# The last down product of a decoder layer: two token parts of 280 and 240 columns, and GpSimd kept out of the second

## The chip, the core and the metric

The kernel runs on one core of one Trainium2 chip, as one launch. The metric is device time in microseconds (us) of that launch, the median of several runs; lower is better. A profiled execution also leaves a trace, whose span runs from the first to the last instruction. The engines are TensorE (PE in the profile, PEld for its weight loads), VectorE (DVE), ScalarE (ACT), GpSimd (POOL) and SyncE (SP), which issues transfers. A queue is shown with a q behind the engine's name.

## The reference, cut to what matters

One layer of a decoder trunk is computed for 512 prompt tokens and 8 sample tokens that share all weights. Its end is the gated feed-forward part and a final norm over the 1024 features:

```python
h2 = rms_norm(x, norm2_g) * (1.0 + sc2) + sh2
gu, up = jnp.split(h2 @ w_ffn_in, 2, axis=-1)
x = x + g2 * ((jax.nn.silu(gu) * up) @ w_ffn_out)
...
y = rms_norm(x, normf_g)      # x / sqrt(mean(x*x) + EPS) * g
```

The gate `g2` is one vector for the prompt and a vector of its own for each of the 8 samples. All is float32.

## The kernel before, in words

Everything is held transposed: features on the 128 partitions, the 520 tokens (512 of the prompt, then 8 samples) along the columns. `x` is eight tiles of 128 features by 520 tokens. Each matrix product is made in a split form: the weights are a high and a low part (`whi`/`wlo`, or `whs`/`wls` where they lie in the general heap), the activations too (`ach`/`acl`), both in the type float32r, and three TensorE matmuls per block of 128 inputs make the product (high by high, low by high, high by low; line 281). A product of 520 columns doesn't fit one bank of PSUM, so the columns are taken in `HALVES` of 260 and 260.

The feed-forward part is done in four sections of inner blocks (`SECT`); the last has five blocks (17 to 21). At its end stands the last down product, `by_halves("fo", ...)` at line 1640: for the half j=0 all eight output tiles i=0..7, then for j=1 all eight. One output tile of one half is 5 x 3 = 15 matmuls, so a half has 120. `begin` and `split_upto` split the weights of the eight units ahead of use, ACT making the high part (line 226) and DVE the low part (line 228).

After each product `fo_done(i, j, b)` follows:

- `residual` adds the gated product to `x`. The first half is one DVE instruction over 260 columns (line 1392). The second half is one over 252 prompt columns (line 1396) and two of 8 columns for the samples (lines 1399 and 1400).
- `sum_squares` squares the new `x` on ACT (line 372; the first tile straight into the sum, line 369) and adds the square to `ss3` on POOL for i below 5, else on DVE (line 373). In the second half the squares of tiles 6 and 7 are not added; TensorE takes them as matmul inputs of their own.
- Where POOL will make the tile's `y`, ACT first scales `x` in place with the norm's weight (line 1494): every tile of the first half, tiles 1, 3 and 5 of the second.

`fo_between(j)` makes the norm of a half. For the first half it is called after the product of tile 0 of the second half: a matmul with ones sums over the partitions (line 380), ACT takes the root (line 381), DVE the reciprocal (line 382), and POOL multiplies all eight tiles (line 1518), with three stores to `yT` (line 1522). For the second half, after the last product: matmuls at line 1509, root at 1510, reciprocal into a PSUM bank at 1512, an ACT copy of it to SBUF at 1513 (GpSimd's products read that copy), five products on DVE (line 1520), three on POOL (line 1518), and four stores. Stores go through SP's queue.

The order on each engine is set by a scheduler that goes by the order of the program text and by what it takes to be ready; each engine then runs its list in order and waits on semaphores. At the end of the kernel each engine drains and all meet at a barrier; the profile books these instructions at line 1691, where the tile context ends.

Of the kernel before, what the change touches and what calls it, by code (L numbers as in the profile page):

```python
# [8 lines left out]
F32 = mybir.dt.float32  # L9
F32R = mybir.dt.float32r  # L10
I32 = mybir.dt.int32
AF = mybir.ActivationFunctionType
ALU = mybir.AluOpType
# [4 lines left out]
D = 1024  # L18
NP = 512
NS = 8  # L20
NT = NP + NS
# [3 lines left out]
KT = 8  # L25
# [2 lines left out]
EPS = 1e-6  # L28
HALF = NT // 2
HALVES = ((0, HALF), (HALF, NT))  # L30

COL_XR, COL_GR, COL_Q, COL_K, COL_V = 0, 1024, 2048, 3072, 4096
COL_FL, COL_GA, COL_GB = 5120, 5136, 6160

P_N1, P_N2, P_NF, P_CW, P_CB, P_BR, P_BI, P_LAM = 0, 1, 2, 3, 7, 8, 9, 10
# [29 lines left out]
def kernel(ctx, tc, xT, par, gates, b_f, cst, cse, own, cache_k, cache_v, cache_lf, pt,  # L65
# [3 lines left out]
    pe, act, dve, pool, sp = nc.tensor, nc.scalar, nc.vector, nc.gpsimd, nc.sync  # L69
# [9 lines left out]
    def slot(name, cols=NT, dt=F32, parts=128):  # L79
        return heap.tile([parts, cols], dt, name=name, tag="slot")  # L80

    def bank(name, parts=128, cols=512):
        return psp.tile([parts, cols], F32, name=name, tag="bank")

    def small(name, parts, cols, bufs=4):
        return sm.tile([parts, cols], F32, name=name, tag="s_" + name, bufs=bufs)
# [6 lines left out]
    x = []  # L93
# [169 lines left out]
    def begin(last=None):  # L263
        n = state["n"]
        state["n"] += 1
        last = len(units) - 1 if last is None else last
        if n < 42:
            tick(KEYS[n], n in VALUES)
        load_chunks(units[reach(n, last, state["load"])][0])
        split_upto(reach(n, last, state["lead"]))  # L270
        flush()
        return n

    def half_product(n, j, a, out):
        hi, lo = splits[n]
        nk = units[n][2]
        t0, t1 = HALVES[j]
        for k in range(nk):
            ah, al = a(k, j) if callable(a) else (v[:, t0:t1] for v in a[k])
            for m, (wt, at) in enumerate(((hi, ah), (lo, ah), (hi, al))):  # L280
                state["mm"] = pe.matmul(out[:, :HALF], lhsT=wt[k], rhs=at, start=k == 0 and m == 0,  # L281
                                        stop=k == nk - 1 and m == 2)

    def run_later(n):
# [81 lines left out]
    def sum_squares(name, f, acc, src, j, eng=dve):  # L366
        t0, t1 = HALVES[j]
        if f == 0:
            act.activation(acc[:, t0:t1], src[:, t0:t1], AF.Square)
        else:  # L370
            q_ = heap.tile([128, HALF], F32, name=name, tag="slot")
            act.activation(q_, src[:, t0:t1], AF.Square)
            eng.tensor_tensor(acc[:, t0:t1], acc[:, t0:t1], q_, ALU.add)  # L373

    def rstd_half(name, ssum, r, j, more=()):
        t0, t1 = HALVES[j]
        ps = bank(f"{name}_{j}")
        parts = [ssum[:, t0:t1], *more]
        for n, q_ in enumerate(parts):
            pe.matmul(ps[:, :HALF], lhsT=ones, rhs=q_, start=n == 0, stop=n == len(parts) - 1)  # L380
        act.activation(r[:, t0:t1], ps[:, :HALF], AF.Sqrt, bias=eps, scale=1.0 / D)
        dve.reciprocal(r[:, t0:t1], r[:, t0:t1])
# [1007 lines left out]
    def residual(f, ps, gate, j):  # L1390
        if j == 0:
            dve.scalar_tensor_tensor(x[f][:, :HALF], ps[:, :HALF], mod[:, gate, f, 0:1], x[f][:, :HALF],
                                     ALU.mult, ALU.add)
            return
        n = NP - HALF
        dve.scalar_tensor_tensor(x[f][:, HALF:NP], ps[:, :n], mod[:, gate, f, 0:1], x[f][:, HALF:NP],  # L1396
                                 ALU.mult, ALU.add)
        t = small("rs", 128, NS)
        dve.tensor_tensor(t, ps[:, n:HALF], mod[:, gate, f, 1:9], ALU.mult)
        dve.tensor_tensor(x[f][:, NP:], x[f][:, NP:], t, ALU.add)  # L1400
# [37 lines left out]
    def by_halves(name, a, done, between):  # L1438
        u = state["n"]
        for j in range(2):  # L1440
            for i in range(KT):
                if j == 0:
                    begin(u + KT - 1)
                b = bank(f"{name}{i}_{j}")
                half_product(u + i, j, a, b)
                done(i, j, b)
                if j == 1 and i == 0:
                    between(0)
                if j == 1 and i < 4 and u + KT < len(units):
                    load_chunks(units[u + KT + i][0])  # L1450
                    split_upto(u + KT + i)
# [24 lines left out]
        t0, t1 = HALVES[j]  # L1476
        dve.tensor_tensor(t[:, t0:t1], b[:, :HALF], t[:, t0:t1], ALU.mult)  # L1477

    tail = []

    def on_pool(f, j):
        return j == 0 or f in (1, 3, 5)

    def fo_done(i, j, b):
        residual(i, b, 5, j)
        if j == 0 or i < 6:
            sum_squares("sq3", i, tail[0], x[i], j, pool if i < 5 else dve)
        else:
            q_ = heap.tile([128, HALF], F32, name="sq3", tag="slot")
            act.activation(q_, x[i][:, HALF:], AF.Square)  # L1490
            squares.append(q_)
        if on_pool(i, j):
            t0, t1 = HALVES[j]
            act.activation(x[i][:, t0:t1], x[i][:, t0:t1], AF.Copy, scale=prm[:, i, P_NF:P_NF + 1])

    squares = []

    def fo_between(j):
        r3 = tail[1]
        t0, t1 = HALVES[j]  # L1500
        r = r3[:, t0:t1]
        if j == 0:
            rstd_half("r3", tail[0], r3, j)
        else:

            ps = bank("r3_1")
            parts = [tail[0][:, t0:t1], *squares]
            for n, q_ in enumerate(parts):
                pe.matmul(ps[:, :HALF], lhsT=ones, rhs=q_, start=n == 0, stop=n == len(parts) - 1)
            act.activation(r, ps[:, :HALF], AF.Sqrt, bias=eps, scale=1.0 / D)  # L1510
            rp = bank("r3p")[:, :HALF]
            dve.reciprocal(rp, r)
            act.copy(r, rp)
        for f0, f1 in ((0, 2), (2, 5), (5, 8)) if j == 0 else ((0, 2), (2, 4), (4, 6), (6, 8)):
            y = pgp.tile([128, 3, HALF], F32, name="y", tag="pg")
            for f in range(f0, f1):
                if on_pool(f, j):
                    pool.tensor_tensor(y[:, f - f0], x[f][:, t0:t1], r, ALU.mult)
                else:
                    dve.scalar_tensor_tensor(y[:, f - f0], x[f][:, t0:t1], prm[:, f, P_NF:P_NF + 1],  # L1520
                                             rp if j else r, ALU.mult, ALU.mult)
            sp.dma_start(yT[128 * f0:128 * f1, t0:t1].rearrange("(f p) t -> p f t", p=128), y[:, :f1 - f0])

    def pair_out():
        return slot("ach", dt=F32R), slot("acl", dt=F32R)
# [75 lines left out]
    for sec, (j0, j1) in enumerate(SECT):  # L1601
        ac = []
        if j0 == 0:
            ts = [slot("sw") for _ in range(PLAIN)]
            ready = []
            u = state["n"]
            for j in range(2):
                for m in range(2 * PLAIN):
                    if j == 0:
                        begin(u + 3)  # L1610
                    b = bank(f"fi{m}_{j}")
                    half_product(u + m, j, h2, b)
                    ready.append((times_up if m % 2 else swish, b, ts[m // 2], j))
                    if j == 0 and m == 0:
                        rstd_half("r2", ss2, r2, 1)
                    if j or m:
                        for fn, *args in ready:
                            fn(*args)
                        ready.clear()
                    if j == 0 and m == 0:  # L1620
                        h2_half(1)
                    first = u + 2 * PLAIN
                    if j == 0:
                        load_chunks(units[first + m][0])
                    elif m:
                        split_upto(first + m - 1)
            for t in ts:
                out = pair_out()
                split_part(out, t)
                ac.append(out)  # L1630
        for jt in range(max(j0, PLAIN), j1):
            if jt == PLAIN:
                for k in range(4):
                    h2_blocks(k)
                defer(0, lambda: split_blocks(0))
                defer(1, lambda: split_blocks(2))
            ac.append((fast_tile if jt in FAST else ffn_tile)(jt))
        if j1 == FF // 128:
            tail += [slot("ss3"), slot("r3")]
            by_halves("fo", ac, fo_done, fo_between)  # L1640
            fo_between(1)
        else:
            for i in range(KT):
                product(f"fo{sec}_{i}", ac, lambda j, b: residual(i, b, 5, j))
# [62 lines left out]
```

## Time and profile before

| | |
|---|---|
| time, median of 3 runs | 1046.94 us (1045.0, 1046.94, 1053.59) |
| time of the profiled execution | 1044.21 us |
| its span | 1042.3 us |
| TensorE clock granted | 0.991 of full speed |
| TensorE busy | 998.9 us (96%) |
| VectorE / ScalarE / GpSimd busy | 777.5 / 533.2 / 304.0 us |

The profiled execution is 1.9 us longer than its span, which lies outside the first and last instruction. Times inside the profile are counted from the start of the span. The chain of waits follows the work that ended last backwards; the timeline lists an engine's instructions in order with start, duration and, in square brackets, the idle time before and what ended it; groups give a mean duration. The ends of matmuls are modelled, so their starts are the better measure.

### The profile page before, as it was taken

How to read it: one execution, taken by the hardware profiler on the slowest of the kernel's cores; microseconds unless marked ns; L12 is line 12 of the kernel's file. 1: busy time of each engine (PE TensorE's matmuls, PEld its weight loads, DVE VectorE, ACT ScalarE, POOL GpSimd, SP SyncE). 2: the span in 40 equal slices, each digit the busy share in tenths (PEclk: the TensorE clock that was granted, in tenths of full speed). 3: DMA queues.
4: the chain of work that ended last, by engine and by line, in shares of the span. 5: the costliest groups of instructions: out<-in, count | busy, mean ns of one | idle time of the engine just before them, and what ended most of it. 6: DMA issues, size and time to landing. Idle time of an engine off the chain costs nothing.

```text
span 1042.3 us, 21246 instructions
## 1 busy us (share of the span) xinstructions
PE 998.9 (96%) x8054; PEld 925.8 (89%) x8054; DVE 777.5 (75%) x1370; ACT 533.2 (51%) x1072; POOL 304.0 (29%) x411
## 2 busy tenths in 40 slices
PE   4999999999999999999999999899999999999993
PEld 1888899999898988878888989899999999999993
DVE  5447999988989978886665546778589558869663
ACT  4523665857671467767793234555244324524451
POOL 0224411112133235654500003472224033223113
PEclk9999999999999999999999999999999999999997
DMA  9898987787889999996766863132343234143212
GB/s 326 295 306 289 300 281 216 262 253 270 263 253 309 321 326 284 303 274 213 263 230 209 282 226 82 41 82 75 100 111 83 91 111 121 54 128 102 75 52 83
DMA packets 165353, 206.97 MB, mean 199 GB/s; under 512 B 9842, under 2 KB 126082, under 8 KB 165186
## 3 DMA queue, kind: packets, MB, share of 16 engines
q1 hardware_dynamic: 148530, 152.52, 47.2%
q0 software_dynamic: 13040, 46.67, 13.5%
q10 hardware_dynamic: 3680, 6.42, 1.7%
q8 instruction: 63, 1.03, 0.4%
q14 instruction: 40, 0.33, 0.1%
HBM read 192.49 MB, written 13.09 MB: 197 GB/s over the span
## 4 chain that ended last, share of the span: by engine, by line
PE 70%; DVE 12%; DMA 7%; ACT 5%; issue 4%; POOL 1%; SPq 0%; POOLq 0%; DVEq 0%; ACTq 0%
PE fo L281 11%; PE fi_S L1578 7%; PE fi_A L1578 5%; PE pb L281 4%; PE gb L281 4%; PE fig L281 4%; PE fiu L281 4%; PE ga L281 3%; PE k L281 3%; PE wo L281 3%; PE v L281 3%; DVE wlo L228 2%; PE gr L281 2%; PE xr L281 2%; DMA wraw<-in_w_in_dram 2%
## 5 line engine op out<-in xcount | busy, mean ns | idle before, releaser
L226 ACT CAST whi<-wraw 128x1024 fp32r<-128x1024 f32 (+2 forms) x113 | 111.4, 987 | 186.1 <-PE fo L281 45.0
L228 DVE TENSOR_TENSOR wlo<-wraw,whi 128x1024 fp32r<-128x1024 f32 (+2 forms) x113 | 137.3, 1216 | 48.6 <-ACT whi L226 40.9
L281 PE MATMUL fo<-ach,whi 128*128 128x260 f32 x302 | 85.6, 283 | 0.0
L281 PE MATMUL fo<-ach,wlo 128*128 128x260 f32 x302 | 85.2, 282 | 0.0
L281 PE MATMUL fo<-acl,whi 128*128 128x260 f32 x302 | 85.0, 282 | 0.0
L658 POOL DMA_DIRECT2D pg<-in_cache_k_dram x74 | 39.4, 533 | 142.4 <-DVE S L707 70.5
L241 POOL TENSOR_TENSOR ws<-wraw 128x512 f32<-128x512 f32 x13 | 20.0, 1538 | 193.5 <-DMA wraw<-in_w_fi_dram 188.7
L706 DVE TENSOR_TENSOR pg<-pg,qb 128x1024 f32<-128x1024 f32 x48 | 58.0, 1227 | 2.4 <-DMA pg<-in_cache_k_dram 2.4
L707 DVE TENSOR_REDUCE S<-pg 128x16 f32<-128x1024 f32 x48 | 57.0, 1207 | 0.1
L281 PEld LDWEIGHTS fo<-ach,whi 128*128 128x128 f32 x302 | 56.8, 188 | 0.2
L281 PEld LDWEIGHTS fo<-ach,wlo 128*128 128x128 f32 x302 | 56.8, 188 | 0.0
L281 PEld LDWEIGHTS fo<-acl,whi 128*128 128x128 f32 x302 | 56.8, 188 | 0.0
L1191 POOL TENSOR_SCALAR p<-p,mu 128x128 f32<-128x128 f32 (+3 forms) x28 | 35.9, 1293 | 48.2 <-DVE mu L1187 31.6
L249 DVE TENSOR_TENSOR wb<-ws,wb 128x512 fp32r<-128x512 f32 x52 | 45.8, 891 | 4.2 <-ACT wb L248 4.1
L373 POOL TENSOR_TENSOR ss<-ss,sq 128x260 f32<-128x260 f32 x18 | 13.7, 761 | 111.3 <-PE ada L344 58.9
L248 ACT CAST wb<-ws 128x512 fp32r<-128x512 f32 x52 | 31.5, 619 | 26.2 <-PE fi_S L1578 8.6
L1185 ACT ACTIVATE p<-p,mu 128x128 f32<-128x128 f32 (+3 forms) x64 | 35.3, 552 | 15.8 <-DVE mu L1184 15.5
L248 ACT CAST wb<-wraw 128x512 fp32r<-128x512 f32 x39 | 23.9, 620 | 34.7 <-PE fo L281 18.1
L1396 DVE SCALAR_TENSOR_TENSOR x<-fo,mod,x 128x252 f32<-128x252 f32 x32 | 15.2, 477 | 32.4 <-PE fo L281 32.4
L1435 ACT CAST ach<-sw 128x260 fp32r<-128x260 f32 (+1 forms) x42 | 17.6, 419 | 41.5 <-DVE sw L1477 22.3
L281 PE MATMUL v<-hh,whi 128*128 128x260 f32 x128 | 37.3, 291 | 1.1 <-DVE pl L1205 1.1
L1578 PE MATMUL fi_S<-twh,wb 128*128 128x260 f32 x208 | 38.1, 282 | 0.0
(435 smaller groups left out, 4065.7 us busy)
## 6 DMA issues: line engine op xcount, KB each, us to landing
araw<-in_ada_w_dram SPq DMA_DIRECT2D x48, 512.0 KB, 6.2
wraw<-in_w_fi_dram SPq DMA_DIRECT2D x44, 512.0 KB, 5.2
pg<-in_cache_k_dram POOLq DMA_DIRECT2D x42, 512.0 KB, 6.2
pg<-in_cache_v_dram SPq DMA_DIRECT2D x42, 512.0 KB, 5.5
wraw<-in_w_in_dram SPq DMA_DIRECT2D x34, 512.0 KB, 7.7
wraw<-in_w_in_dram SPq DMA_DIRECT2D x11, 1024.0 KB, 10.3
pg<-in_cache_v_dram POOLq DMA_DIRECT2D x22, 512.0 KB, 6.4
pg<-in_cache_k_dram POOLq DMA_DIRECT2D x32, 256.0 KB, 5.7
```

The source lines that it names most:

```text
L226: state["act"] = act.copy(hi[:, :k1 - k0], src)
L228: state["last"] = dve.tensor_tensor(lo[:, :k1 - k0], src, hi[:, :k1 - k0].bitcast(F32), ALU.subtract)
L241: pool.tensor_tensor(s1, a21, a22, ALU.add)
L248: state["act"] = act.copy(t[:, :4], src)
L249: state["last"] = dve.tensor_tensor(t[:, 4:], src, t[:, :4].bitcast(F32), ALU.subtract)
L281: state["mm"] = pe.matmul(out[:, :HALF], lhsT=wt[k], rhs=at, start=k == 0 and m == 0, stop=k == nk - 1 and m == 2)
L658: done.append(eng.dma_start(pg, cache[bass.ds(r, 1), :, c0:c1].rearrange("a p c -> (a p) c")))
L706: dve.tensor_tensor(pg, pg, q, ALU.mult)
L707: last = dve.tensor_reduce(S[r // 2][:, c:c + H], pg.rearrange("p (h d) -> p h d", d=DH), AX.X, ALU.add)
L1185: act.activation(p[:, :n + 128], p[:, :n + 128], AF.Exp, bias=mu[:, 0:1], scale=-1.0, accum_out=mu[:, 1:2])
L1191: (pool.tensor_scalar(p, p, mu[:, 2:3], None, ALU.mult) if a and i + 1 < KT else act.activation(p, p, AF.Copy, scale=mu[:, 2:3]))
L1578: state["mm"] = pe.matmul(b, lhsT=wt[k], rhs=at, start=k == 0 and m == 0, stop=k == 3 and m == 2)
```

## The change

The last down product gets a function of its own, `last_product`, in place of `by_halves`, `fo_done` and `fo_between`. Its two parts are columns 240 to 519 (280 columns, the samples among them) and then columns 0 to 239. In the first part the residual has the two sample instructions; in the second it is one instruction. Squares of the first part are added as before (POOL for tiles 1 to 4, DVE for 5 to 7); in the second part DVE adds those of tiles 1 to 5, and 6 and 7 go to TensorE as before. ACT scales `x` for all tiles in both parts. The norm of the first part is called at the same place and has its eight products on POOL; the norm of the second part has all eight products on DVE, which reads the reciprocal from PSUM, and the ACT copy is gone. Groups of tiles per store stay the same.

```diff
+LAST_PARTS = ((240, NT), (0, 240))
...
     def half_product(n, j, a, out):
+        part_product(n, *HALVES[j], (lambda k: a(k, j)) if callable(a) else a, out)
+
+    def part_product(n, t0, t1, a, out):
...
-                state["mm"] = pe.matmul(out[:, :HALF], lhsT=wt[k], rhs=at, ...
+                state["mm"] = pe.matmul(out[:, :t1 - t0], lhsT=wt[k], rhs=at, ...
...
+    def last_product(ac):
+        ss3, r3 = slot("ss3"), slot("r3")
+        squares = []
+        u = state["n"]
+
+        def done(i, j, t0, t1, b):
+            gate, n = mod[:, 5, i], min(t1, NP) - t0
+            if j == 0:
+                t = small("rs", 128, NS)
+                dve.tensor_tensor(t, b[:, n:t1 - t0], gate[:, 1:9], ALU.mult)
+            dve.scalar_tensor_tensor(x[i][:, t0:t0 + n], b[:, :n], gate[:, 0:1], x[i][:, t0:t0 + n],
+                                     ALU.mult, ALU.add)
+            if j == 0:
+                dve.tensor_tensor(x[i][:, NP:], x[i][:, NP:], t, ALU.add)
+            if i == 0:
+                act.activation(ss3[:, t0:t1], x[i][:, t0:t1], AF.Square)
+            else:
+                q_ = heap.tile([128, t1 - t0], F32, name="sq3", tag="slot")
+                act.activation(q_, x[i][:, t0:t1], AF.Square)
+                if j == 0 or i < 6:
+                    (pool if j == 0 and i < 5 else dve).tensor_tensor(ss3[:, t0:t1], ss3[:, t0:t1], q_, ALU.add)
+                else:
+                    squares.append(q_)
+            act.activation(x[i][:, t0:t1], x[i][:, t0:t1], AF.Copy, scale=prm[:, i, P_NF:P_NF + 1])
+
+        def norm(j, t0, t1):
+            n = t1 - t0
+            ps = bank(f"r3_{j}")[:, :n]
+            parts = [ss3[:, t0:t1], *squares]
+            for k, q_ in enumerate(parts):
+                pe.matmul(ps, lhsT=ones, rhs=q_, start=k == 0, stop=k == len(parts) - 1)
+            act.activation(r3[:, t0:t1], ps, AF.Sqrt, bias=eps, scale=1.0 / D)
+            r = bank("r3p")[:, :n] if j else r3[:, t0:t1]
+            dve.reciprocal(r, r3[:, t0:t1])
+            eng = dve if j else pool
+            for f0, f1 in ((0, 2), (2, 4), (4, 6), (6, 8)) if j else ((0, 2), (2, 5), (5, 8)):
+                y = pgp.tile([128, 3, n], F32, name="y", tag="pg")
+                for f in range(f0, f1):
+                    eng.tensor_tensor(y[:, f - f0], x[f][:, t0:t1], r, ALU.mult)
+                sp.dma_start(yT[128 * f0:128 * f1, t0:t1].rearrange("(f p) t -> p f t", p=128), y[:, :f1 - f0])
+
+        for j, (t0, t1) in enumerate(LAST_PARTS):
+            for i in range(KT):
+                if j == 0:
+                    begin(u + KT - 1)
+                b = bank(f"fo{i}_{j}")
+                part_product(u + i, t0, t1, ac, b)
+                done(i, j, t0, t1, b)
+                if j and i == 0:
+                    norm(0, *LAST_PARTS[0])
+        norm(1, *LAST_PARTS[1])
...
         if j1 == FF // 128:
-            tail += [slot("ss3"), slot("r3")]
-            by_halves("fo", ac, fo_done, fo_between)
-            fo_between(1)
+            last_product(ac)
```

More of the change, by code (lines that the diff above doesn't have):

```diff
@@ L274, in half_product @@
     def half_product(n, j, a, out):
+        part_product(n, *HALVES[j], (lambda k: a(k, j)) if callable(a) else a, out)
+    def part_product(n, t0, t1, a, out):
         hi, lo = splits[n]
         nk = units[n][2]
-        t0, t1 = HALVES[j]
         for k in range(nk):
-            ah, al = a(k, j) if callable(a) else (v[:, t0:t1] for v in a[k])
+            ah, al = a(k) if callable(a) else (v[:, t0:t1] for v in a[k])
             for m, (wt, at) in enumerate(((hi, ah), (lo, ah), (hi, al))):
-                state["mm"] = pe.matmul(out[:, :HALF], lhsT=wt[k], rhs=at, start=k == 0 and m == 0,
+                state["mm"] = pe.matmul(out[:, :t1 - t0], lhsT=wt[k], rhs=at, start=k == 0 and m == 0,
                                         stop=k == nk - 1 and m == 2)
@@ L1477, in times_up @@
         dve.tensor_tensor(t[:, t0:t1], b[:, :HALF], t[:, t0:t1], ALU.mult)
[L1479 to L1493, printed above, removed]
-            act.activation(x[i][:, t0:t1], x[i][:, t0:t1], AF.Copy, scale=prm[:, i, P_NF:P_NF + 1])
@@ L1496 @@
[L1496 to L1522, printed above, removed]
```

## The prediction, as put on record before the changed kernel ran

> **What bounds the kernel now.** I read the page first, then the chain of waits, then who waited for whom on SP, then the timeline of the last 50 us, engine by engine.
>
> ```profile
> PE 998.9 (96%) x8054; PEld 925.8 (89%) x8054; DVE 777.5 (75%) x1370; ACT 533.2 (51%) x1072; POOL 304.0 (29%) x411
> ```
>
> TensorE sets the pace of the whole. The change touches only the last 47 us, and there the chain of waits reads:
>
> ```profile
> 995.09 16.23 PE fo L281 x135
> 1011.32 0.44 PE r L380 x2
> 1017.94 3.57 POOL y L1518 x5
> 1030.45 0.77 POOLq L1691
> 1031.22 1.38 POOL y L1518 x2
> ```
>
> Here the chain leaves TensorE: from 1016 on it runs through GpSimd, and it ends in GpSimd's closing instructions at line 1691. The second thing to see is how the kernel closes:
>
> ```profile
> L1691 SPq DRAIN  x3: 7/7/7, 1036.7 to 1041.7; - x3
> L1691 POOLq DRAIN  x3: 46/104/10986, 1030.5 to 1042.0; - x3
> L1691 DVEq DRAIN  x2: 19/1061/2103, 1030.5 to 1041.7; - x2
> SPq L1691 <- PEq L1691: 5.4, 2, 4.9
> SPq L1691 <- DMA out_yT_dram<-y: 2.1, 1, 2.1
> ```
>
> SP has seen the last store land and drains at 1036.7. Then it sits 4.9 us. What is still running is GpSimd's drain: issued at 1030.45, 10.99 us long, so over at 1041.44; only then do the engines meet, and 0.84 us later the span ends. DVE's drain, queued at the same 1030.5 behind its own products, lasts only 2.10 us, just as long as those products. The row puts SP's wait down to TensorE's queue, but TensorE and DVE were done long before. So the stores are **not** the last wait now: GpSimd's drain is, and it stands behind GpSimd's last product.
>
> The arithmetic before that, in the order in which it ends:
>
> ```profile
> 1024.09 0.28 PE L281 MATMUL fo<-acl,whs 128*128 128x260 f32 x1
> 1021.44 3.22 POOL L373 TENSOR_TENSOR ss<-ss,sq 128x260 f32<-128x260 f32 x4
> 1024.70 0.43 DVE L373 TENSOR_TENSOR ss<-ss,sq 128x260 f32<-128x260 f32 x1 [3.11 <-POOL ss L373]
> 1025.71 0.47 DVE L1396 SCALAR_TENSOR_TENSOR x<-fo,mod,x 128x252 f32<-128x252 f32 x1
> 1026.29 0.17 DVE L1400 TENSOR_TENSOR x<-x,rs 128x8 f32<-128x8 f32 x1
> 1026.48 0.42 ACT L1490 ACTIVATE sq<-x 128x260 f32<-128x260 f32 x1 [0.24 <-DVE x L1400]
> 1026.30 1.37 PE L1509 MATMUL r<-sq,cs 128*128 128x260 f32 x4 [0.41 <-ACT sq L1490]
> 1028.21 1.79 DVE L1512 RECIPROCAL r3p<-r 128x260 f32<-128x260 f32 x1 [1.76 <-ACT r L1510]
> 1030.44 2.07 DVE L1520 SCALAR_TENSOR_TENSOR y<-x,prm,r3p 128x260 f32<-128x260 f32 x5 [0.44 <-ACT r L1513]
> 1030.48 2.12 POOL L1518 TENSOR_TENSOR y<-x,r 128x260 f32<-128x260 f32 x3 [5.82 <-ACT r L1513]
> L1522 SPq DMA_DIRECT2D out_yT_dram<-y x7: 372/372/445, 1017.3 to 1033.1; - x7
> DMA to landing us min/median/max: 2.2/2.6/2.8
> ```
>
> TensorE's last product ends at 1024.37, but its residual starts only at 1025.71: DVE stood 3.11 us at a sum that waited for GpSimd, whose four sums came after its eight products of the first half. From 1024.37 to GpSimd's last y at 1032.60 is 8.23 us.
>
> **The change part by part.**
>
> *TensorE.* The column total is the same, in widths of 280 and 240 for 260. What a width costs is read from spacings of starts:
>
> ```profile
> 355.90 0.19 PEld L1178 LDWEIGHTS sc<-ksA,qlA 128*128 128x128 f32 x1
> 356.01 0.19 PEld L1177 LDWEIGHTS sc<-ksB,qqB 128*128 128x128 f32 x1
> 356.07 0.27 PE L1177 MATMUL sc<-ksB,qqB 128*128 128x128 f32 x1
> 356.18 0.28 PE L1178 MATMUL sc<-ksB,qlB 128*128 128x128 f32 x1
> ...
> 409.60 0.39 PE L1234 MATMUL po<-ph,v 128*128 128x512 f32 x1
> 409.83 0.40 PE L1234 MATMUL po<-pl,v 128*128 128x512 f32 x1
> 410.07 0.34 PE L1234 MATMUL po<-ph,v 128*128 128x384 f32 x1
> ...
> 550.48 0.22 PE L1234 MATMUL po<-ph,v 128*128 128x128 f32 x1
> 550.53 0.28 PE L1234 MATMUL po<-pl,v 128*128 128x128 f32 x1
> ```
>
> All of these are float32r like the product in question. 512 columns take (410.07 - 409.60) / 2 = 0.235; 260 take 16.23 / 135 = 0.120. The slope is 0.115 / 252 = 0.00046 a column, so 280 take 0.129 and 240 take 0.111. At 128 columns the spacing is 0.11, the same as that of the weight loads, so 0.11 is the floor and 240 lies on it. Twice 120 matmuls: 120 x (0.129 + 0.111) = 28.8, against 240 x 0.120 = 28.8: **0**. The other end: were the 0.11 at 128 columns the stream and not the load, 240 would take 0.206, which is +11.4. I take the floor, because a 128-column matmul whose weights were there already gave way to the next after 0.05 (550.48 to 550.53).
>
> A rule that speaks against the change here: the Trainium skill, "TensorE: Matmul & The Clock Gate", LDWEIGHTS, has a load take its columns over 1.2 GHz (107 ns for 128), and Back-to-back issue gap has N / 2.4 + 2.5 ns for a matmul alone, so below 250 columns the load would be the limit; by it the sum would be 120 x (119.2 + 106.7 - 2 x 110.8) = +0.5 us. The measured 0.120 at 260 is above its 110.8, and the measurement decides.
>
> *First part.* Two DVE instructions of 8 columns per tile move here from the second. They meet TensorE nowhere but at the seam, where the norm's matmul needs the sum of tile 7.
>
> ```profile
> 1004.55 0.88 DVE L228 TENSOR_TENSOR wls<-wraw,whs 128x512 fp32r<-128x512 f32 x2
> 1009.57 0.49 DVE L1392 SCALAR_TENSOR_TENSOR x<-fo,mod,x 128x260 f32<-128x260 f32 x1 [0.39 <-PE fo L281]
> 1010.55 0.43 DVE L373 TENSOR_TENSOR ss<-ss,sq 128x260 f32<-128x260 f32 x1 [0.49 <-ACT sq L372]
> L1400 DVE TENSOR_TENSOR x<-x,rs 128x8 f32<-128x8 f32 x8 | 2.5, 314 | 0.2
> L1518 POOL TENSOR_TENSOR y<-x,r 128x260 f32<-128x260 f32 x11 | 7.8, 748 | 15.6 <-DVE rs L1399 9.8 <-ACT r L1513 5.8
> 668.85 1.46 DVE L1419 TENSOR_TENSOR h2r<-x,r 128x260 f32<-128x260 f32 x4
> ```
>
> The last weight split ends at 1005.43, and tile 7, which needs it, starts at 995.09 + 7 x 15 x 0.120 = 1007.7 now, with 0.129 at 1008.6. Eight tiles of two adds at 0.31 at most are 5 us of DVE spread over 15.5 us, and some of it falls into DVE's waits; the cover of 2 to 3 us hides the rest. Without it TensorE would wait for each split, some 0.6 a tile. At the seam, residual to sum takes 1.41 now (1009.57 to 1010.98); with 280 columns 1.52, and with two adds of 0.17 before the square about 1.7 in all, as they overlap it in part. TensorE reaches the norm's matmul one tile later, after 15 x 0.111 = 1.67, less the drain of the last matmul: I book a stall of **+0.3** (bounds 0 and 0.5). The first part's reciprocal is 1.79 x 280/260 = 1.93 and, after the sum at about 1012.3, the matmuls (0.7) and the root (0.5), ends near 1015.6; it holds up only residuals, which have slack.
>
> *GpSimd.* It loses four sums and three products at the end. Five products of 260 took 3.57 in the chain, 0.714 each, so eight of 280 take 8 x 0.77 = 6.1 from 1015.7: done near 1021.8. The upper end: the mean of line 1518 (0.748, so 0.806) and four waits for a DVE sum of 0.40 make 8.05, done at 1023.8. Its drain, which stood 1041.44 - 1032.60 = 8.84 behind its last product, would end at 1030.6 to 1032.6.
>
> *DVE in the second part.* Per tile a residual (0.45) and for tiles 1 to 5 a sum (0.40), where TensorE needs 1.67: it fits. The 8-column add of the samples took 0.314 on average, most of it beside GpSimd's products, and 0.17 at 1026.29 with GpSimd idle, so sums will be held up now and then. If each of tiles 1 to 4 lost a whole GpSimd product (0.77), I get the last residual 0.3 late; with no contention 0. I take 0, since tiles 6 and 7 have no sum and give the slack back. The Trainium skill, "SBUF — State Buffer", Who interferes with whom, says that a DVE instruction with two SBUF inputs and a reading GpSimd one exclude each other for a whole instruction; by it the upper end would hold, 0.3 more. The row of the 8-column add agrees in kind.
>
> *The end.* TensorE ends at 1024.37 + 0.3 = 1024.7. Residual 0.46 (no sum before it, no sample instructions behind): 1025.2. Square 0.40: 1025.6. Matmuls 0.73 (0.77 from 1026.90 to 1027.67, by width): 1026.35. Root 0.50 (0.54 from 1027.67 to 1028.21): 1026.85. Reciprocal 1.79 x 240/260 = 1.65: 1028.5. The copy (0.44 with its gaps) is gone. Eight DVE products: the four at 668.85 took 0.365 each, so 8 x 0.337 = 2.7; by the row of line 1520, 0.414 each, 3.1. I take 2.7, the same operation: **1031.25** against 1032.60. The last store is issued at 1031.3 instead of 1033.1 (now two groups become ready at once, and the second waits out the 0.37 of the first). It takes 2.2 to 2.8 to land; now 2.6, behind three others in quick succession, and I take 2.4 with wider spacing: 1033.7 instead of 1035.7, **2.0** earlier. SP's closing waits take the same 1.0: SP drains at 1034.7. GpSimd's drain is over by then, at 1032.6 at the latest, so the meeting point moves from 1041.44 to 1034.7: **-6.75**, of which 2.0 is the shorter arithmetic and 4.75 is SP's wait for the drain.
>
> The profiled execution, 1044.21, becomes 1037.5. It lay 2.7 under the median of its three runs, so on that median: 1046.94 - 6.75 = **1040.2**. With the bounds (stall, contention, products, landing) the gain is 5.7 to 7.2: 1039.7 to 1041.2.
>
> **The rivals.**
>
> *The drain keeps its place behind the stores.* There is one such drain in the trace, and it ends 5.7 after the last landing as well as 8.84 after the last product. If it hangs on the stores, only the 2.0 remains: **1044.9**. For it: nothing separates the two in one trace. Against it: it was issued at 1030.45, before any of the last four stores.
>
> *Narrow matmuls stream slower.* Every long product of this kernel has 260 columns; the trace has none between 128 and 256. If below 256 the stream ran at half rate, the second part takes +11.4 and the end moves by 11.4 - 6.75 = +4.65: **1051.6**. It turns slower from 0.111 + 6.75 / 120 = 0.167 per matmul. At the price of a plain float32 product (two instructions, 0.44 at 260, so 0.41 at 240) it is +35.4: **1075.6**. Against both stands the 0.05 at line 1234, against the second also the 0.11 at 128 columns.
>
> *DVE falls behind.* The sums, contended, and a reciprocal in their midst leave the last residual late, or GpSimd's products stretch until its drain passes 1034.7. Each us late costs one; 2 us gives **1042.2**.
>
> **How the numbers follow.** Forecast 0.74; drain with the stores 0.13; narrow matmuls 0.07 (half rate 0.04, float32 price 0.03); DVE or GpSimd late 0.06. The range goes from the profiled execution with the largest gain, 1044.21 - 7.2 = 1037.0, less 1 for the scatter of runs (1044.21, 1045.0 and 1046.94 are a like set), so 1036.0, to the median with nothing gained, 1047.0; it holds all but the narrow-matmul cases, and the rest left out is the spread of the runs, 1045.0 to 1053.59. The bound of 1% (10.5 us) is about what a measurement of this kernel can tell from no change. The forecast is 0.64% and stays inside it; runs at the low end could pass it: faster 0.05. Slower by over 1% only the float32 price, and a half rate with slow runs: 0.04. The same: 0.91.
>
> **What would show it.** The spacing of the second part's matmuls near 0.111; GpSimd's last product near 1022 and its drain over before SP's; SP's wait of 4.9 at line 1691 gone, with the last landing now the last wait; the last residual within 0.1 of TensorE's end; DVE's eight products in 2.7 to 3.1; no copy between reciprocal and products. I am wrong if GpSimd's drain still ends last, or if the spacing is 0.16 or more.

## The result, and the profile after

| | before | with the change |
|---|---|---|
| median time, ten runs of each | 1048.35 us | 1041.21 us |
| lowest to highest | 1045.0 to 1053.7 us | 1037.69 to 1044.35 us |
| span of the profiled execution | 1042.3 us | 1042.0 us |
| first matmul of the last product | 994.92 us | 1000.87 us |
| from there to the end of the span: the **stretch** | 47.38 us | 41.13 us |

The ratio of the times is 0.9929, with a 95% interval of 0.9908 to 0.9951: 0.7% faster, where 0.64% was forecast (1040.2 us). The 6.25 us that the stretch lost are 0.6% and lie inside that interval; the times can't tell them from the 6.75 that were forecast.

The spans of the two profiled executions are nearly the same, and that has to be read rightly. Runs of one kernel scatter by 7 to 9 us, and the executions that were profiled differ by 6 us long before the edit. The rows of the last-product matmuls show it: the first line is of before, the second of after, and the low-part matmuls of the first section began at 728.9 and at 734.8.

```profile
L281 PE MATMUL fo<-ach,wlo x302: 277/282/288, 728.9 to 1014.9; 128*128 128x260 f32 x151
```

```profile
L284 PE MATMUL fo<-ach,wlo x302: 271/282/296, 734.8 to 1022.2; 128*128 128x260 f32 x136, 128*128 128x280 f32 x8, 128*128 128x240 f32 x7
```

So from here on the stretch is compared, in which the changed code runs; it is the span less the start of the last product's first matmul. These are the two first matmuls, before and after:

```profile
994.92 0.28 PE L281 MATMUL fo<-ach,whi 128*128 128x260 f32 x1
1000.87 0.29 PE L284 MATMUL fo<-ach,whi 128*128 128x280 f32 x1
```

In the stretch the chain of waits after the change is this (start, duration, what):

```profile
1001.03 17.42 PE fo L284 x135
1018.45 0.10 issue
1018.55 0.71 PE r L1512 x2
1019.26 11.80 PE fo L284 x105
1031.05 0.02 issue
1031.08 0.48 DVE x L1492
1031.55 0.02 issue
1031.58 0.41 ACT sq L1500
1031.99 0.04 issue
1032.03 0.69 PE r L1512 x2
1032.72 0.02 issue
1032.74 0.47 ACT r L1513
1033.21 0.02 issue
1033.23 1.67 DVE r3p L1515
...
1035.65 1.89 DVE y L1520 x6
```

GpSimd is gone from it. The last residual follows TensorE's end after 0.03, where it was 1.34 before, and each link waits only for the one ahead. The close (instructions at the line where the tile context ends, SP's waits, and GpSimd's products):

```profile
L1699 POOLq DRAIN  x3: 46/104/15614, 1022.3 to 1041.7; - x3
L1699 SPq DRAIN  x3: 7/7/7, 1041.1 to 1041.4; - x3
SPq L1699 <- DMA out_yT_dram<-y: 2.2, 1, 2.2
SPq L1699 <- PEq L1699: 0.7, 2, 0.5
1022.30 6.75 POOL L1520 TENSOR_TENSOR y<-x,r 128x280 f32<-128x280 f32 x8 [7.59 <-DVE r L1515]
```

GpSimd's drain is issued at 1022.3, lasts 15.61 and is over at 1037.9, 8.86 after its last product (1029.05). SP drains at 1041.1, the 4.9 us that it sat before are now 0.5, and the last wait of any length is the landing of the last store.

### The profile page after: what moved, and what is told of

The parts are those of the page before. It is cut to its first block, busy times and chain, and to the rows that moved or that the text cites. A ratio compares the mean times of both kernels' runs of the same rounds, so it can differ in the third digit from the quotient of the medians.

```text
span 1042.0 us, 21242 instructions
## 1 busy us (share of the span) xinstructions
PE 1003.5 (96%) x8054; PEld 929.2 (89%) x8054; DVE 778.8 (75%) x1377; ACT 535.1 (51%) x1076; POOL 302.1 (29%) x404
## 4 chain that ended last, share of the span: by engine, by line
PE 78%; DVE 10%; DMA 5%; ACT 4%; issue 2%; POOL 1%; SPq 0%; DVEq 0%; ACTq 0%; POOLq 0%
PE fo L284 12%; PE fi_S L1588 7%; PE fi_A L1588 5%; PE pb L284 4%; PE gb L284 4%; PE v L284 4%; PE fig L284 4%; PE fiu L284 4%; PE k L284 4%; DMA wraw<-in_w_in_dram 3%; PE ga L284 3%; PE pa L284 3%; PE wo L284 3%; PE gr L284 2%; PE pv L794 2%; PE xr L284 2%
## 5 line engine op out<-in xcount | busy, mean ns | idle before, releaser
L284 PE MATMUL fo<-ach,whi 128*128 128x260 f32 (+2 forms) x302 | 85.6, 284 | 0.0
L284 PE MATMUL fo<-ach,wlo 128*128 128x260 f32 (+2 forms) x302 | 85.2, 282 | 0.0
L284 PE MATMUL fo<-acl,whi 128*128 128x260 f32 (+2 forms) x302 | 85.0, 283 | 0.0
L1588 PE MATMUL fi_A<-h2h,wb 128*128 128x260 f32 x208 | 37.9, 282 | 0.0
L284 PE MATMUL pb<-oh,whi 128*128 128x260 f32 x128 | 36.7, 287 | 1.0 <-ACT oh L1295 1.0
```

Source lines behind the costliest of these rows:

```text
L284: state["mm"] = pe.matmul(out[:, :t1 - t0], lhsT=wt[k], rhs=at, start=k == 0 and m == 0, stop=k == nk - 1 and m == 2)
L1588: state["mm"] = pe.matmul(b, lhsT=wt[k], rhs=at, start=k == 0 and m == 0, stop=k == 3 and m == 2)
```

## The experiments

All stretches in one table; the sections below say how each was meant. Ratios are to the kernel before, run beside it on the same chip. Each stretch comes from one trace, and spans are read to 0.1 us, so differences of 0.1 in it mean nothing. Starts agree better where the code is the same: TensorE's last product starts 29.17 after its first in the kernel before, e2, e3, e5 and e9, and 29.89 and 29.90 after it with the change and in e1.

| kernel | first matmul | span | stretch | expected | ratio of times, interval |
|---|---|---|---|---|---|
| before | 994.92 | 1042.3 | 47.38 | | |
| after | 1000.87 | 1042.0 | 41.13 | | 0.9929, 0.9908 to 0.9951 |
| e1, GpSimd late | 999.19 | 1045.8 | 46.61 | 46.5 | 0.9993, 0.9975 to 1.0011 |
| e2, products only | 1000.88 | 1043.3 | 42.42 | 42.7 | 0.9951, 0.9933 to 0.9970 |
| e3, sums only | 998.07 | 1044.1 | 46.03 | 46.1 | 0.9996, 0.9981 to 1.0012 |
| e4, 260 and 260 | 997.94 | 1039.0 | 41.06 | 41.1 to 41.3 | 0.9943, 0.9924 to 0.9961 |
| e5, both in halves | 998.94 | 1040.0 | 41.06 | 41.1 | 0.9945, 0.9925 to 0.9964 |
| e6, 320 and 200 | 999.19 | 1042.0 | 42.81 | 42.2 | 0.9956, 0.9939 to 0.9973 |
| e7, late norm | 998.40 | 1040.2 | 41.80 | 40.85 | 0.9941, 0.9924 to 0.9958 |
| e8, equal, late norm | 996.04 | 1037.0 | 40.96 | 40.7 | 0.9931, 0.9914 to 0.9949 |
| e9, halves, plain products | 997.02 | 1038.0 | 40.98 | 40.6 | 0.9921, 0.9893 to 0.9949 |

**e1: one small GpSimd instruction put back.**

```diff
-        norm(1, *LAST_PARTS[1])
+        y = norm(1, *LAST_PARTS[1])          # norm returns its last y tile
+        pool.tensor_copy(small("late", 128, NS), y[:, 1, :NS])
```

> The changed kernel with one more GpSimd instruction: a copy of 8 columns of the last y tile into an unused small tile. It stands behind DVE's last product and nothing waits for it. The stretch counted here and below runs from the first matmul of the last product to the end of the span: 47.4 us before the change, 41.1 after. Theory (GpSimd's closing drain ends a fixed 8.86 us after GpSimd's last instruction, and the kernel can't end earlier): that copy ends near 36.8 us of the stretch, the drain near 45.7, the stretch becomes 46.5, so +5.4 on the changed kernel; SP waits about 4.5 us at the close again. Rival (the drain is tied to the stores or to the other engines): the stretch stays 41.1.

The rows of GpSimd's last instruction and of the close:

```profile
1035.92 0.19 POOL L1534 COPY late<-y 128x8 f32<-128x8 f32 x1 [8.56 <-DVE y L1520]
L1701 POOLq DRAIN  x3: 46/104/9046, 1035.9 to 1045.5; - x3
SPq L1701 <- PEq L1701: 6.1, 2, 5.6
```

A copy of 0.19 us that nobody waits for takes the stretch to 46.61, 5.48 more than the change alone, and the time back to that of the kernel before. The drain ends at 1035.9 + 9.05 = 1044.95, 8.84 after the copy, and SP, which drained at 1039.5, waits for it. The theory is shown; the rival, by which the stretch stays at 41.1, falls.

**e2 and e3: the change's two moves off GpSimd, each alone in the kernel before.**

```diff
 # e2
-        return j == 0 or f in (1, 3, 5)
+        return j == 0
...
-            act.copy(r, rp)
 # e3
-            sum_squares("sq3", i, tail[0], x[i], j, pool if i < 5 else dve)
+            sum_squares("sq3", i, tail[0], x[i], j, pool if j == 0 and i < 5 else dve)
```

> The kernel before with one part of the change: the second half's eight products of y all on DVE (which reads the reciprocal from PSUM; the ACT copy and the three scalings of x are gone). Halves, samples and GpSimd's late sums stay. Theory: GpSimd's last instruction is its last sum at 29.7 us of the stretch, its drain ends at 38.6 and the stores decide: DVE's eight products (0.41 each) start 0.4 us earlier and end near 38.3, last landing near 40.9, stretch 42.7, so a gain of 4.7 with no shorter arithmetic. Rival (the gain comes from the sums that no longer hold up DVE): the stretch stays within 0.5 of 47.4.

> The kernel before with the other part: the second half's sums of tiles 1 to 4 on DVE; three of its products of y stay on GpSimd. Theory: DVE no longer stands at a sum (3.1 us before), the last residual follows TensorE's end within 0.1, everything behind it comes 1.3 us earlier, and GpSimd's drain, 8.86 behind its last product, still ends last: stretch 46.1. Rival (arithmetic is what was bought): the stretch falls by most of the 6.3, below 43.

In e2 GpSimd ends with its sums, and its drain runs beside the last chain:

```profile
1027.42 3.21 POOL L373 TENSOR_TENSOR ss<-ss,sq 128x260 f32<-128x260 f32 x4
1036.01 3.26 DVE L1519 SCALAR_TENSOR_TENSOR y<-x,prm,r3p 128x260 f32<-128x260 f32 x8
L1690 POOLq DRAIN  x3: 46/104/9611, 1029.9 to 1043.0; - x3
L1690 SPq DRAIN  x3: 7/7/7, 1042.4 to 1042.7; - x3
```

GpSimd's drain ends at 1039.5, and SP, whose drain stands behind the last landing, only gets to it at 1042.4: the stores decide, and the stretch is 4.96 shorter, although DVE now makes eight products instead of five and the last residual is as late as before. In e3 the arithmetic is repaired and the close is not:

```profile
1027.56 0.48 DVE L1396 SCALAR_TENSOR_TENSOR x<-fo,mod,x 128x252 f32<-128x252 f32 x1 [0.42 <-PE fo L281]
1032.35 2.13 POOL L1518 TENSOR_TENSOR y<-x,r 128x260 f32<-128x260 f32 x3 [6.85 <-ACT r L1513]
L1691 POOLq DRAIN  x3: 46/104/10996, 1032.3 to 1043.9; - x3
SPq L1691 <- PEq L1691: 5.4, 2, 4.9
```

The last residual now comes 0.04 behind TensorE's last product (1027.24 + 0.28), 1.3 earlier than before, and SP sits its 4.9 as before: 1.35 shorter. The time can't tell e3 from the kernel before; the stretch can.

**e5: both moves, halves and samples untouched.** The edits of e2 and e3 together.

> The kernel before with both parts of the second and third run together: second half's sums of tiles 1 to 4 and all its products on DVE, copy gone; the halves stay 260 and 260 and the samples stay in the second. Theory (the whole gain is GpSimd's absence at the end; widths and samples cancel): TensorE's last product starts 29.17 after the first as before (no longer seam), the residual with the samples' two adds follows at once, and the stretch is 42.42 less the 1.35 that the sums were worth: 41.1, the same as with the change. Rival (widths and samples are worth something at the end): 41.6 or more.

41.06: as short as with the whole change (41.13). The new widths, the samples' move into the first part and the plain products are in sum worth nothing at the end; 4.96 + 1.35 = 6.31 is the whole of the 6.25. They cancel: with the change TensorE's last product starts 0.72 later than in e5 (29.89 and 29.17 after the first), and from there to the first of the last four stores it takes 4.92 instead of 5.57.

**e4 and e6: the widths.**

```diff
-LAST_PARTS = ((240, NT), (0, 240))
+LAST_PARTS = ((260, NT), (0, 260))   # e4
+LAST_PARTS = ((200, NT), (0, 200))   # e6
```

> The changed kernel with parts of 260 and 260 columns (samples in the first, GpSimd out of the second). It tells what the widths 280 and 240 are worth. Theory: on TensorE nothing but the seam: 15 matmuls of 0.120 instead of 0.112 take 1.80, so the wait of 0.28 at the norm's matmul is gone and TensorE ends some 0.4 earlier; the last part's chain is 20 columns longer, +0.5 (reciprocal 0.13, eight products 0.2, the rest 0.15). Stretch 41.1 to 41.3. Rival (a narrow last part is what helps): 42 or more. If narrow matmuls cost more than their columns, the stretch falls well below 41.

> The changed kernel with parts of 320 and 200 columns. Theory (weight loads set a floor of 0.110 per matmul): first part 0.149 each, second 0.110 to 0.112; TensorE's last product starts 31.8 after the first instead of 29.89, the last part's chain is 40 columns shorter (-0.8), stretch 42.2. Rival (time goes by columns at every width): 0.094 each in the second part, TensorE as now, stretch 40.3. Second rival (narrow matmuls run at a lower rate): over 0.13 each, stretch above 44.

e4 came out as expected in sum, but not by the way told: the norm's matmul still made TensorE wait (its last product starts 29.59 after the first, not the 29.5 that I wanted and not the 29.17 of before), since the samples' adds stand before the last square. That wait is 0.16 of the 0.42 over 29.17 (across the norm's matmul 0.84, before 0.68); the rest arises near the start of the first part, by a wait that is told below. In e6 the floor is seen directly. The first spacing here is that of a matmul whose successor's weights were ready, the next ones are of the stream:

```profile
1017.07 0.26 PE L284 MATMUL fo<-ach,whi 128*128 128x200 f32 x1
1017.16 0.28 PE L284 MATMUL fo<-ach,wlo 128*128 128x200 f32 x1
1017.27 0.28 PE L284 MATMUL fo<-acl,whi 128*128 128x200 f32 x1
1017.39 0.27 PE L284 MATMUL fo<-ach,whi 128*128 128x200 f32 x1
```

0.09 once, then 0.11 and 0.12: 200 columns are paid like 240. Neither rival holds. Of the 0.6 over the expected 42.2, 0.35 is TensorE, whose last product starts 32.15 after the first and not 31.8; about half of that arises at the norm's matmul, across which it takes 1.22 and with the change 1.05. The other 0.2 lies behind it: the residuals of tiles 6 and 7 come back to back, as in e7, and from TensorE's last start to SP's drain it is 0.6 shorter than with the change, not 0.8.

**e7 and e8: the seam.**

```diff
-                if j and i == 0:
+                if j and i == 1:
                     norm(0, *LAST_PARTS[0])
```

> The changed kernel with the first part's norm called one tile later (after tile 1 of the second part). Theory: TensorE no longer waits 0.28 at the norm's matmul and ends that much earlier, GpSimd's products end 1.4 to 1.7 later, its drain at about 38.6 of the stretch, still before SP's closing drain near 40.0: stretch 40.85. Rival (GpSimd's drain is passed on): 41.1 or more. A gain of 0.3 us is below what the times can show; the stretch can.

> Parts of 260 and 260 with the samples in the first, and the norm called one tile later. Theory: the wait of 0.39 that the equal parts showed at the seam goes: stretch 40.7, and the time is that of the changed kernel or 0.4 less. Rival: the wait returns elsewhere (the reciprocal now stands before later residuals), stretch 41.0 or more.

e7 missed. TensorE did end earlier (last start 29.54 after the first, 29.89 with the change), but the stretch is 0.67 longer. GpSimd's drain had no part in it (over at 1038.0, SP's at 1039.3), so the rival has the number without the cause. GpSimd's products began 24.0 after the first matmul instead of 21.4, 2.6 later and not the 1.4 to 1.7 that I had allowed, and DVE's sums met them up to tile 5:

```profile
1027.70 0.82 DVE L1502 TENSOR_TENSOR ss<-ss,sq 128x240 f32<-128x240 f32 x1 [0.47 <-ACT sq L1500]
1028.44 0.83 DVE L1492 SCALAR_TENSOR_TENSOR x<-fo,mod,x 128x240 f32<-128x240 f32 x2
1029.77 0.39 ACT L1500 ACTIVATE sq<-x 128x240 f32<-128x240 f32 x1
```

The residuals of tiles 6 and 7 come back to back, the last one at 1028.8 for a product that ended at 1028.2; its square then waits behind ACT's scaling of tile 6 and starts only at 1029.77. That is the third rival of the prediction, DVE falling behind, brought about by a delay of 2.6 us. In e8, with 260 columns, GpSimd's products are shorter and the chain held; but it missed too: it gained 0.1 on e4, not 0.4, and 40.96 lies nearer the rival's 41.0 than 40.7. Only 0.14 of TensorE's lateness went; 0.28 is left (29.45 after the first, before 29.17), none of it at the norm's matmul, and TensorE's weight queue again shows the wait of 0.2 in the first part.

**e9: the best of the parts.**

```diff
 # on e5
-        if on_pool(i, j):
+        if True:
...
-                    dve.scalar_tensor_tensor(y[:, f - f0], x[f][:, t0:t1], prm[:, f, P_NF:P_NF + 1],
-                                             rp if j else r, ALU.mult, ALU.mult)
+                    dve.tensor_tensor(y[:, f - f0], x[f][:, t0:t1], rp, ALU.mult)
```

> The kernel of e5_both_in_halves, with ACT scaling x for all eight tiles of the second half and DVE's products as plain ones of two tensors, as the change has them. It is to be the shortest close: halves and samples as before (so no seam, TensorE's last start at 29.17), GpSimd out, plain products. Theory: e5's eight products took 3.26 (0.41 each), plain ones of 260 columns took 2.77 in e4: stretch 41.06 - 0.5 = 40.6, against 41.13 with the change. Rival (the scalings hold up ACT's last square): 41.0 or more. In the times both are the same as the changed kernel's.

The products did shrink, from 3.26 to 2.77, but the stretch by less than 0.1. The rival isn't the cause: the last square starts 1.11 after TensorE's last start in both. The first two lines are of e9; the last two are the last four stores, of e5 and then of e9:

```profile
1030.85 2.77 DVE L1519 TENSOR_TENSOR y<-x,r3p 128x260 f32<-128x260 f32 x8
SPq L1689 <- DMA out_yT_dram<-y: 2.1, 1, 2.1
1033.68 2.75 SPq L1521 DMA_DIRECT2D out_yT_dram<-y  x4
1031.64 2.38 SPq L1520 DMA_DIRECT2D out_yT_dram<-y  x4
```

SP's wait for the last landing is 2.1 here and was 1.7 in e5, so 0.4 of 0.5 is given back there. The stores tell why. SP drains 5.5 after the first of the four is issued in e5 (1039.2) and 5.6 in e9 (1037.2), and 5.4 to 5.5 in the kernel before, the changed one, e2 and e4, whatever the products take. In e5 and e9 alike the DMA engines are busy for about 3.0 us almost without a break with the four, 1.07 MB, which is about 0.75 a store. A pair of products takes 0.82 in e5 and 0.69 in e9: with the slower ones the transfers keep pace, with the faster ones they set the end, and what was gained is only that the first store comes 0.12 sooner. It has the lowest ratio of all (0.9921), but its interval covers that of the change, so it isn't shown to be faster.

## Why the prediction was right, point by point

- **The drain.** Predicted to end 8.84 behind GpSimd's last product; measured 8.86. In e1, e2 and e3 it is 8.84, 8.88 and 8.82 behind a copy, a sum and a product. With the change it ended at 1037.9, 3.2 before SP's, so the rival that tied it to the stores (1044.9) is refuted by the changed kernel itself and by e2; e1 shows that GpSimd's last instruction moves it.
- **The shares.** 4.75 for the drain and 2.0 for the arithmetic were forecast. SP drains 40.23 after the first matmul instead of 41.78, so 1.55 for the arithmetic and the stores; the span ends 0.9 after that instead of 5.6, so 4.7 for the drain. The two moves measured alone give 4.96 and 1.35; they don't split quite like the terms, since in e2 the stores end earlier too.
- **The size.** 6.75 forecast, 6.25 in the stretch. The step that was mis-sized is TensorE: booked +0.3 for the stall at the seam, measured 29.89 against 29.17 for the last start, so +0.72. That is three terms. Across the norm's matmul it took 1.05 (1018.16 to 1019.21) and before 0.68, so the seam cost 0.37, of which TensorE stood 0.28: inside the bounds. The spacings were 0.129 as booked (102 of them from 1003.46 to 1016.60) and 0.112 for 0.111, which makes 0.1. And a wait was missed, which cost 0.26 and which TensorE's weight queue names:

```profile
PEld r L1512 <- PE fo L284: 0.3, 1, 0.3
PEld fo L284 <- DVE acl L1439: 0.2, 1, 0.2
1002.62 0.42 DVE L1439 TENSOR_TENSOR acl<-sw,ach 128x260 fp32r<-128x260 f32 x1
1002.81 0.29 PE L284 MATMUL fo<-ach,wlo 128*128 128x280 f32 x1
1003.10 0.53 PE L284 MATMUL fo<-acl,whi 128*128 128x280 f32 x2
1003.46 0.29 PE L284 MATMUL fo<-ach,whi 128*128 128x280 f32 x1
```

  The first part now has columns 240 to 519, and the last 260 of them are the part of the inner activations that is finished last: TensorE had only just made them (its product of `fiu` ended at 1001), and DVE's low part (`acl`) was done at 1003.04. From 1002.81 to 1003.46, three spacings took 0.65 instead of 0.39. The same wait of 0.2 stands in e4 and e8, where the first part is the second half, and there is none where the halves keep their old order. I looked for what each operation costs and not for which columns are ready first.
- **The last chain.** From TensorE's last start to the last product of `y`: forecast 6.83, measured 6.77 (1030.76 to 1037.53). The eight products took 2.60, forecast 2.7. The stores took 3.6 from there to SP's drain, forecast 3.45.
- **Narrow matmuls.** No penalty at 240 or 200 columns: 0.112 and 0.11. The floor is the pace of the weight loads, which also start 0.11 apart there (1017.07, 1017.18 and 1017.29 in e6). The Trainium skill, "TensorE: Matmul & The Clock Gate", LDWEIGHTS, puts such a load at 107 ns for 128 columns, 3 to 5 ns under what is seen here.
- **DVE beside GpSimd.** Predicted to be held up and to recover by tile 7. It was so:

```profile
1022.98 0.41 DVE L1502 TENSOR_TENSOR ss<-ss,sq 128x240 f32<-128x240 f32 x1 [0.47 <-ACT sq L1500]
1027.58 0.81 DVE L1502 TENSOR_TENSOR ss<-ss,sq 128x240 f32<-128x240 f32 x1 [0.47 <-ACT sq L1500]
1028.32 0.45 DVE L1492 SCALAR_TENSOR_TENSOR x<-fo,mod,x 128x240 f32<-128x240 f32 x1
1029.24 0.41 DVE L1502 TENSOR_TENSOR ss<-ss,sq 128x240 f32<-128x240 f32 x1 [0.47 <-ACT sq L1500]
1031.08 0.47 DVE L1492 SCALAR_TENSOR_TENSOR x<-fo,mod,x 128x240 f32<-128x240 f32 x1 [1.04 <-PE fo L284]
```

  Three of the four sums beside GpSimd's products take 0.81 or 0.82; the first of them (1022.98) and the one after the products, which end at 1029.05, take 0.41. The residuals, which read one operand from PSUM, don't stretch: 0.45. The Trainium skill, "SBUF — State Buffer", Who interferes with whom, says that a DVE instruction with two inputs in SBUF contends with a GpSimd one that reads SBUF, and one with a single such input doesn't; the trace agrees in kind. GpSimd's products paid too: 6.75 for eight where 6.1 was forecast, and at 260 columns 6.52 in e3 and e5, with the sums beside them, against 5.68 before. Tiles 6 and 7 gave the slack back: DVE stood 1.04 before the last residual. The delay of 2.6 in e7 was more than that.

## What to carry to other kernels

Look at what ends the span before costing the arithmetic ahead of it: the closing drain that stands behind GpSimd's last instruction is part of GpSimd's price, and here it was three quarters of the gain (4.7 of 6.25). Share work with GpSimd in the middle of a kernel, not so late that this drain ends after the last store. And when tokens are taken in another order, ask which columns are finished first, and compare the changed stretch, not whole spans, where the rest of the kernel scatters by more than the gain.

## What the runs showed of the hardware that was not expected

GpSimd's first drain at the end is over 8.8 to 8.9 us after GpSimd's last instruction in all eleven kernels, behind a product, a sum or a copy of 0.19 us, while DVE's lasts just as long as DVE's own products; the two later drains of GpSimd take 0.1 and 0.05. What it does in that time no run here shows. The end of four stores in quick succession follows the first of them: SP drains 5.4 to 5.6 us after its issue with 0.98 to 1.07 MB in all, whether the products behind them take 0.41 each (e5) or 0.35 (e9).
